# Large sums and scalings of an attention moved from GpSimd to DVE and ACT, and the emptying of two kinds of blocks put first in the plan

## The chip, the cores and the metric

One core of one Trainium2 chip. The metric is the device time of one execution in microseconds; the kernel before takes 782.17 us (median of 3 runs, 782.04 to 782.22).

## The reference

Two pre-norm residual layers on 256 positions of width 2048, then a final norm. The first layer is sliding-window attention (window 128, 32 query heads on 4 key/value heads, a learned sink per head in the softmax's denominator). The second has three attention branches on one set of queries: over 15 compressed blocks, over selected blocks (with 256 positions all blocks are selected), and over a window that covers all positions; each branch's result is weighted with a sigmoid gate per head. Both multiply the attention's output with a SiLU gate before the output projection.

```python
for i in range(DEPTH):                      # DEPTH = 2
    h = rmsnorm(x, norm_w[i])
    out = mixer_a(...) if i == 0 else mixer_b(...)
    x = x + out
return rmsnorm(x, final_norm_w)

# mixer_a, per head:  e = exp(s - m);  p = e / (sum(e) + exp(sink - m));  o = p @ v
# mixer_b, per head:  o = g0 * o_cmp + g1 * o_slc + g2 * o_win,  g = sigmoid(gates)
# both:               out = (o * silu(z)) @ w_out
```

## The kernel before

The kernel is written as two layers of code. `trunk` records every operation into a `Plan` and emits nothing. `Plan.order` then simulates the five engines with a price for each operation (`_price`) and a latency between engines, and sends each engine, whenever it is free in that simulation, the ready operation with the smallest `i - early`, where `i` is the place in the program. `early` is normally 0; `FIRST` puts an operation before all normal ones, `LAST` behind them. The order found in this way is the order of the instructions in each engine's queue, and on the chip each engine works through its queue in that order, waiting by semaphores. The prices know nothing of one engine holding up another. All recorded operations therefore have one line in the profile (L217, the call in `emit`), and they are told apart by the names of their tiles.

The projections are 234 weight blocks ("steps"), each a 128x1024 tile of weights. SP loads it (`raw`, 4 buffers), ACT rounds it to a high part (`w_hi`), DVE subtracts to get the low part (`w_lo`, 3 buffers each; both recorded as FIRST in `split`), and TensorE multiplies activations with the parts in three passes into one of three PSUM banks (`acc`; the matmuls are recorded as LAST, so that they fill what attention leaves). When a block of columns is done, a function empties its bank. For queries that is `post_q` (L636): ACT copies the bank to `q` with a scale, GpSimd rotates the first quarter of the head's width (`rope`). For gates it is `post_z` (L687): ACT copies one half of the bank to `side`, DVE adds it to the other half and writes `u`; from `u` a tanh and products make the SiLU gate. A bank is free for the next block when these have read it.

Attention runs beside the projections, one unit per head group (4) and tile of 128 positions (`t`, 2): a front part (transposing queries, scores, softmax) and a back part (transposing probabilities, products with the values), each cut into pieces. `background` runs pieces after each half step, against a credit that grows by a rate per half step; the rates stand in one list by stage (L1331). A unit has two parities of heads (`par`), each with four heads in one tile `sm` (128 x 4 x 256).

In the first layer (`a_scores`, L753), per unit and parity: scores (`s`) go through DVE (mask and maximum), ACT takes the exponential and its sum, DVE adds the sink's part (`es`) to `den` and takes the reciprocal. For `t` = 1 GpSimd then adds the two halves of `sm`, and for both `t` GpSimd multiplies by `den`. In the back part for `t` = 1 DVE multiplies the transposed probabilities with two masks (`pt<-pT,part`). In the second layer (`b_scores`, L1176) there are two such tiles per unit and parity, one per branch: after the exponentials, the reciprocal and the product with the gates (`denb`), DVE scales the first branch's tile and GpSimd the second's. The compressed branch's softmax (`cmp_softmax`, L1215) runs on DVE and ACT, with one product on GpSimd (`sc`), and gives `pc`. TensorE transposes `sm` into `pT`, and ACT or DVE copies that to `pt`.

Of the kernel before, what the change touches and what calls it, by code (L numbers as in the profile page):

```python
# [17 lines left out]
OP = mybir.AluOpType  # L18
AX = mybir.AxisListType

P = 128
# [10 lines left out]
FIRST, LAST = 1 << 20, -(1 << 20)  # L32
# [307 lines left out]
def trunk(ctx: ExitStack, tc: tile.TileContext, x, final_norm_w, a_w_in, a_w_out, b_w_in, kc_pos, kc_w1, kc_w2, vc_pos, vc_w1, vc_w2,  # L340
          b_w_out, consts, small, xT, out):
    nc = tc.nc
    plan = Plan()
    PE, ACT, DVE, POOL, SP = (Engine(plan, n, e) for n, e in (
        ("PE", nc.tensor), ("ACT", nc.scalar), ("DVE", nc.vector), ("POOL", nc.gpsimd), ("SP", nc.sync)))
# [7 lines left out]
    def s_bank(name):  # L353
        return pp.tile([P, NB], F32, tag="s", name=name, bufs=2)
# [7 lines left out]
    def copy(out, in_, scale=1.0):  # L362
        return ACT.activation(out, in_, AF.Copy, scale=scale)
# [258 lines left out]
    def rope(v, t, nh):  # L622

        tmp = sb.tile([P, 2, HPG, 16], F32, tag="rope", name="rope")
        a, b = tmp[:, 0, 0:nh, :], tmp[:, 1, 0:nh, :]

        def bc(tab, lo, n):
            return tab[:, t].rearrange("p a b -> p (a b)")[:, None, lo:lo + n].to_broadcast([P, nh, n])
        POOL.tensor_tensor(out=a, in0=v[:, :, 0:16], in1=bc(cs, 0, 16), op=OP.mult)
        POOL.tensor_tensor(out=b[:, :, 0:8], in0=v[:, :, 8:16], in1=bc(sn, 0, 8), op=OP.mult)  # L630
        POOL.tensor_tensor(out=b[:, :, 8:16], in0=v[:, :, 0:8], in1=bc(sn, 8, 8), op=OP.mult)
        POOL.tensor_tensor(out=v[:, :, 0:16], in0=a, in1=b, op=OP.add)
# [3 lines left out]
    def post_q(layer, g):  # L636
        def post(t, ps):
            q = sb.tile([P, NB], F32, tag="q", name="q", bufs=4)
            copy(q, ps, scale=rq[layer][:, t:t + 1])
            rope(q.rearrange("p (h d) -> p h d", d=HD), t, HPG)  # L640
            qs[layer, g, t] = q
            flags.add(("q", layer, g, t))
        return post
# [43 lines left out]
    def post_z(layer, g, part):  # L687
        def post(b, ps):
            if part == b == 0:
                us[layer, g] = sb.tile([P, 4, S], F32, tag="u", name="u", bufs=2)  # L690
            u = us[layer, g][:, 2 * part + b, :]
            side = sb.tile([P, S], F32, tag="q32", name="side", bufs=2)
            copy(side, ps[:, S:2 * S])
            DVE.tensor_tensor(u, ps[:, 0:S], side, op=OP.add)
            if b == 0:
                return
            u = us[layer, g][:, 2 * part:2 * part + 2, :]
            DVE.tensor_tensor(u, u, rbc[:, None, :].to_broadcast([P, 2, S]), op=OP.mult)
            th = sb.tile([P, 2, S], F32, tag="q32", name="th", bufs=2)
            ACT.activation(th, u, AF.Tanh)  # L700
            DVE.scalar_tensor_tensor(u, th, 1.0, u, op0=OP.add, op1=OP.mult)
            if part == 1:
                flags.add(("z", layer, g))
                urgent.extend(gated(layer, g, *held) for held in late.pop((layer, g), []))
        return post
# [21 lines left out]
    def gated(layer, g, t, pv, aT):  # L727
        u = us[layer, g][:, :, t * P:(t + 1) * P]
        DVE.tensor_tensor(u, u, pv, op=OP.mult)
        hi = aT[0][:, 4 * g:4 * g + 4, t * P:(t + 1) * P]  # L730
        copy(hi, u)
        DVE.tensor_sub(aT[1][:, 4 * g:4 * g + 4, t * P:(t + 1) * P], u, hi)
        flags.add(("a", layer, g, t))
        yield 0.0
# [18 lines left out]
    def a_scores(g, t, kT, qT, par, sm, nm, den):  # L753
        n = (t + 1) * P
        mk = mflat[:, 2 * P:2 * P + n]
        for i0 in (0, 2):
            ps = s_bank("s")
            for i in (i0, i0 + 1):
                o = ps[:, (i - i0) * S:(i - i0 + 1) * S]
                q = qT[:, 2 * i + par, :]  # L760
                if t == 0:

                    PE.matmul(o.rearrange("p (a b) -> p a b", a=2), q, kT[:, g, :, P:2 * P], start=True, stop=True)
                else:
                    for hl in range(2):
                        PE.matmul(o, q, kT[:, g, hl, 0:S], start=hl == 0, stop=hl == 1)
            if t == 0:
                sides = ps.rearrange("p (i a b) -> p i a b", i=2, a=2)
                low = sb.tile([P, 512], F32, tag="q32", name="low", bufs=2)[:, 0:2 * P].rearrange("p (i b) -> p i b", i=2)
                DVE.tensor_tensor(low, sides[:, :, 1, :], mk[:, None, :].to_broadcast([P, 2, P]), op=OP.add)  # L770
            for i in (i0, i0 + 1):
                h = g * HPG + 2 * i + par
                src, other = (sides[:, i - i0, 0, :], low[:, i - i0, :]) if t == 0 else (
                    ps[:, (i - i0) * S:(i - i0 + 1) * S], mk)
                DVE.tensor_tensor_reduce(out=sm[0][:, i, 0:n], in0=src, in1=other,
                                         scale=-1.0, scalar=nsink[:, h:h + 1], op0=OP.add, op1=OP.min,
                                         accum_out=nm[:, i:i + 1])
                ACT.activation(sm[0][:, i, 0:n], sm[0][:, i, 0:n], AF.Exp, scale=-1.0,
                               bias=nm[:, i:i + 1], accum_out=den[:, i:i + 1])
            yield 220.0 * (t + 1)  # L780
        es = sb.tile([P, 4], F32, tag="es", name="es", bufs=2)
        h0 = g * HPG + par
        DVE.tensor_tensor(es, nm, sinks[:, h0:h0 + 7:2], op=OP.add)
        ACT.activation(es, es, AF.Exp)
        DVE.tensor_tensor(den, den, es, op=OP.add)
        DVE.reciprocal(den, den)
        p = sm[0][:, :, 0:P]
        if t:

            POOL.tensor_tensor(out=p, in0=p, in1=sm[0][:, :, P:2 * P], op=OP.add)  # L790
        POOL.tensor_tensor(out=p, in0=p, in1=den[:, :, None].to_broadcast([P, 4, P]), op=OP.mult)
        yield 0.0

    def p_transposed(sms, br, off, k):
# [106 lines left out]
    nA = len(steps)  # L901
# [35 lines left out]
    nA_out = len(steps)  # L937
# [236 lines left out]
    nB = len(steps)  # L1174

    def b_scores(g, t, qT, par, sm, nm, den, sc):  # L1176
        kT = lay["kT"]
        for i in range(4):
            h = 2 * i + par
            if t == 0:  # L1180
                spans = [(128, 272)]
            else:
                spans = [(0, 272), (272, 256)]
            banks = []
            for off, n in spans:
                ps = s_bank("s")
                banks.append(ps)
                for hl in range(2):
                    PE.matmul(ps[:, 0:n], qT[:, h, :], kT[:, g, hl, off:off + n], start=hl == 0, stop=hl == 1)
            if t == 0:  # L1190
                parts = [(banks[0][:, 0:P], mflat[:, 0:P]), (banks[0][:, 144:272], mflat[:, 0:P])]
                pc = banks[0][:, P:P + 16]
            else:
                parts = [(banks[0][:, 0:S], mflat[:, 0:S]), (banks[1][:, 0:S], mflat[:, P:P + S])]
                pc = banks[0][:, S:S + 16]
            n = (t + 1) * P
            for br, (src, mk) in enumerate(parts):
                DVE.tensor_tensor_reduce(out=sm[br][:, i, 0:n], in0=src, in1=mk, scale=-1.0, scalar=-NEG,
                                         op0=OP.add, op1=OP.min, accum_out=nm[:, br, i:i + 1])
                if br == 0:  # L1200
                    DVE.tensor_tensor(sc[:, h, :], pc, mask_c[:, t, :], op=OP.add)
                ACT.activation(sm[br][:, i, 0:n], sm[br][:, i, 0:n], AF.Exp, scale=-1.0,
                               bias=nm[:, br, i:i + 1], accum_out=den[:, br, i:i + 1])
            yield 230.0 * len(spans)
        DVE.reciprocal(den, den)
        h0 = g * HPG + par
        DVE.tensor_tensor(den, den, lay["gate"][:, t, 1:3, h0:h0 + 7:2], op=OP.mult)
        n = (t + 1) * P
        for br in range(2):
            eng = POOL if br else DVE  # L1210
            eng.tensor_tensor(out=sm[br][:, :, 0:n], in0=sm[br][:, :, 0:n],
                              in1=den[:, br, :, None].to_broadcast([P, 4, n]), op=OP.mult)
        yield 0.0

    def cmp_softmax(g, t, sc):  # L1215
# [104 lines left out]
    n = len(steps)  # L1320
# [7 lines left out]
    hT_pair(0, hT0, 0)  # L1328
    for i in range(AHEAD):
        split(steps[i])  # L1330
    rates = [(0, 450.0), (nA, 900.0), (nA + 8, 600.0), (nA_out, 750.0), (nB, 1200.0)]  # L1331
    for i, st in enumerate(steps):
        for start, r in rates:
            if i == start:
# [77 lines left out]
```

## Time and profile before

| | us |
|---|---|
| median of 3 runs | 782.17 (782.04 to 782.22) |
| the profiled execution | 782.04 |
| its span, first to last instruction | 780.0 |
| TensorE (PE) busy | 766.9 |
| DVE busy | 569.6 |
| ACT busy | 469.9 |
| GpSimd (POOL) busy | 124.4 |

The granted clock of TensorE is 0.998 of full speed over the span. Matmuls are pipelined: a matmul's duration in the timeline includes the time in which its results drain, during which the next has begun, so that the time that a matmul really takes is the distance from its start to the next one's. An idle time in brackets is the engine's own, before the instruction, with what ended it. Repeated buffers of a tile carry one name.

### The profile page before, as it was taken

The numbers are of one execution on the slowest core, as the hardware profiler recorded it, in microseconds if no ns is written. First come the engines' busy times: TensorE is split into PE (matmuls) and PEld (weight loads), VectorE is DVE, ScalarE is ACT, GpSimd is POOL, SyncE is SP. The second block draws the span as 40 slices with busy tenths as digits, with TensorE's granted clock in tenths as the row PEclk, the third lists the DMA queues.
The fourth block names the chain that finished last, engine by engine and source line by source line (L and its number), as shares of the span: only waits on it lengthen the run. The fifth ranks groups of instructions, "written<-read, shape, count | busy, mean of one in ns | idle before, by whom it ended". The sixth has DMA issues, their size and how long they took to land.

```text
span 780.0 us, 11584 instructions
## 1 busy us (share of the span) xinstructions
PE 766.9 (98%) x3992; PEld 623.6 (80%) x3992; DVE 569.6 (73%) x1159; ACT 469.9 (60%) x950; POOL 124.4 (16%) x170
## 2 busy tenths in 40 slices
PE   8999999999999999999999999999999999999995
PEld 6888688787787788888888888878878887868884
DVE  6649959869779655565776579969969798965562
ACT  6857557457466445544666477667657866845442
POOL 1112112113023000020101021311232411111110
PEclk9999999999999999999999999999999999999999
DMA  9763563654554555676687653545445352454642
GB/s 326 242 207 117 162 187 111 171 181 133 164 163 134 181 184 182 186 200 171 182 245 238 176 163 109 163 113 159 122 122 149 107 158 102 135 190 155 195 164 108
DMA packets 86475, 129.73 MB, mean 166 GB/s; under 512 B 6323, under 2 KB 43234, under 8 KB 86289
## 3 DMA queue, kind: packets, MB, share of 16 engines
q1 hardware_dynamic: 85792, 127.42, 54.0%
q0 software_dynamic: 336, 1.29, 0.5%
q8 instruction: 31, 0.51, 0.3%
q10 hardware_dynamic: 288, 0.30, 0.1%
q14 instruction: 28, 0.22, 0.1%
HBM read 126.89 MB, written 2.10 MB: 165 GB/s over the span
## 4 chain that ended last, share of the span: by engine, by line
PE 83%; DVE 12%; issue 4%; DMA 1%; ACT 0%; ACTq 0%; POOLq 0%; POOL 0%; SPq 0%; DVEq 0%
PE acc L217 68%; PE pv L217 4%; DVE w_lo L217 3%; PE s L217 3%; PE pT L217 3%; DVE sm L217 3%; DVE den L217 2%; DVE u L217 1%; PE mlp L217 1%; DVE qT L217 1%; PE qT L217 1%; PE gates L217 1%; PE xT L217 1%; DMA raw<-in_a_w_in 1%; DVE pt L217 1%
## 5 line engine op out<-in xcount | busy, mean ns | idle before, releaser
L217 DVE TENSOR_TENSOR w_lo<-raw,w_hi 128x1024 fp32r<-128x1024 f32 (+1 forms) x231 | 297.0, 1288 | 141.0 <-ACT w_hi L217 137.9
L217 ACT ACTIVATE w_hi<-raw 128x1024 fp32r<-128x1024 f32 (+1 forms) x231 | 241.1, 1048 | 161.4 <-PE acc L217 123.6
L217 PE MATMUL acc<-w_hi,hT 128*128 128x512 f32 x768 | 244.4, 395 | 1.7 <-DVE u L217 1.0
L217 PE MATMUL acc<-hT,w_hi 128*128 128x512 f32 x512 | 185.0, 397 | 0.0
L217 PEld LDWEIGHTS acc<-w_hi,hT 128*128 128x128 f32 x768 | 142.2, 188 | 33.2 <-issue 2.4
L217 PE MATMUL acc<-w_lo,hT 128*128 128x512 f32 x384 | 150.4, 394 | 0.0
L217 PE MATMUL acc<-hT,w_lo 128*128 128x256 f32 x512 | 144.8, 285 | 0.0
L217 PEld LDWEIGHTS acc<-hT,w_hi 128*128 128x128 f32 x512 | 96.2, 188 | 18.1
L217 PEld LDWEIGHTS acc<-hT,w_lo 128*128 128x128 f32 x512 | 96.6, 189 | 0.7
L217 PE MATMUL acc<-w_hi,aT_hi 128*128 128x512 f32 x236 | 92.5, 393 | 0.3 <-DVE kTB L217 0.3
L217 PE MATMUL acc<-w_hi,aT_lo 128*128 128x512 f32 x236 | 92.6, 392 | 0.0
L217 PE MATMUL acc<-w_lo,aT_hi 128*128 128x512 f32 x236 | 92.1, 391 | 0.0
L217 PEld LDWEIGHTS acc<-w_lo,hT 128*128 128x128 f32 x384 | 72.0, 188 | 13.5
L217 ACT ACTIVATE sm<-sm,nmb 128x128 f32<-128x128 f32 (+1 forms) x128 | 56.7, 444 | 18.7 <-DVE nmb L217 15.4
L217 POOL TENSOR_TENSOR sm<-sm,denb 128x512 f32<-128x512 f32 (+1 forms) x16 | 31.5, 1966 | 142.3 <-DVE mx L217 32.8
L217 PEld LDWEIGHTS acc<-w_hi,aT_hi 128*128 128x128 f32 x236 | 44.2, 188 | 9.9 <-DVE kTB L217 0.8
L217 PEld LDWEIGHTS acc<-w_hi,aT_lo 128*128 128x128 f32 x236 | 44.3, 188 | 9.7 <-issue 0.8
L217 PEld LDWEIGHTS acc<-w_lo,aT_hi 128*128 128x128 f32 x236 | 44.3, 188 | 8.9
L217 DVE CUSTOM_DVE_ANT_0 sm<-s,mask 128x128 f32<-128x128 f32 (+1 forms) x128 | 42.7, 348 | 10.1 <-PE s L217 9.6
L217 PE MATMUL pT<-ident,sm 128*128 128x128 f32 x256 | 38.2, 274 | 0.6 <-DVE sm L217 0.6
L217 PEld LDWEIGHTS s<-kTB,qT 128*128 128x128 f32 x192 | 31.9, 188 | 8.2 <-issue 3.1
L217 PE MATMUL s<-kTB,qT 128*128 128x272 f32 x192 | 38.3, 295 | 0.0
(188 smaller groups left out, 864.5 us busy)
## 6 DMA issues: line engine op xcount, KB each, us to landing
raw<-in_b_w_in SPq DMA_DIRECT2D x88, 512.0 KB, 3.7
raw<-in_a_w_in SPq DMA_DIRECT2D x71, 512.0 KB, 3.7
raw<-in_a_w_out SPq DMA_DIRECT2D x32, 512.0 KB, 3.8
raw<-in_b_w_out SPq DMA_DIRECT2D x32, 512.0 KB, 4.5
x<-in_x SPq DMA_DIRECT2D x8, 256.0 KB, 7.1
raw<-in_b_cmp_k_w SPq DMA_DIRECT2D x4, 512.0 KB, 3.7
raw<-in_b_cmp_v_w SPq DMA_DIRECT2D x4, 512.0 KB, 4.1
out<-x SPq DMA_DIRECT2D x4, 512.0 KB, 3.1
```

Source lines behind the costliest of these rows:

```text
L217: return getattr(eng.real, method)(*[real(a) for a in args], **{k: real(a) for k, a in kw.items()})
```

## The change

Four things. (1) In the first layer's softmax the sum of the two halves (8 times) and the multiplication by `den` (16 times) are issued on DVE instead of GpSimd. (2) In the second layer the scaling of the second branch's tile, one GpSimd operation for four heads (16 times), becomes four ACT copies with a scale, one per head, in place. (3) In `post_q` and `post_z` the operations that empty the bank (ACT's copy to `q`; ACT's copy to `side` and DVE's sum to `u`) are recorded as FIRST. (4) The credit rate between the first layer's output projection and the second's is 800 instead of 750.

```diff
     def post_q(layer, g):
         def post(t, ps):
             q = sb.tile([P, NB], F32, tag="q", name="q", bufs=4)
+            plan.early = FIRST
             copy(q, ps, scale=rq[layer][:, t:t + 1])
+            plan.early = 0
             rope(q.rearrange("p (h d) -> p h d", d=HD), t, HPG)
...
             side = sb.tile([P, S], F32, tag="q32", name="side", bufs=2)
+            plan.early = FIRST
             copy(side, ps[:, S:2 * S])
             DVE.tensor_tensor(u, ps[:, 0:S], side, op=OP.add)
+            plan.early = 0
             if b == 0:
                 return
...
         p = sm[0][:, :, 0:P]
         if t:
 
-            POOL.tensor_tensor(out=p, in0=p, in1=sm[0][:, :, P:2 * P], op=OP.add)
-        POOL.tensor_tensor(out=p, in0=p, in1=den[:, :, None].to_broadcast([P, 4, P]), op=OP.mult)
+            DVE.tensor_tensor(out=p, in0=p, in1=sm[0][:, :, P:2 * P], op=OP.add)
+        DVE.tensor_tensor(out=p, in0=p, in1=den[:, :, None].to_broadcast([P, 4, P]), op=OP.mult)
         yield 0.0
...
         n = (t + 1) * P
-        for br in range(2):
-            eng = POOL if br else DVE
-            eng.tensor_tensor(out=sm[br][:, :, 0:n], in0=sm[br][:, :, 0:n],
-                              in1=den[:, br, :, None].to_broadcast([P, 4, n]), op=OP.mult)
+        DVE.tensor_tensor(out=sm[0][:, :, 0:n], in0=sm[0][:, :, 0:n],
+                          in1=den[:, 0, :, None].to_broadcast([P, 4, n]), op=OP.mult)
+        for i in range(4):
+            copy(sm[1][:, i, 0:n], sm[1][:, i, 0:n], scale=den[:, 1, i:i + 1])
         yield 0.0
...
-    rates = [(0, 450.0), (nA, 900.0), (nA + 8, 600.0), (nA_out, 750.0), (nB, 1200.0)]
+    rates = [(0, 450.0), (nA, 900.0), (nA + 8, 600.0), (nA_out, 800.0), (nB, 1200.0)]
```

## Rows read from the trace of the kernel before

**Rows 1.** The page's part 1: engine, busy us, share of the span, instructions.
```profile
PE 766.9 (98%) x3992; PEld 623.6 (80%) x3992; DVE 569.6 (73%) x1159; ACT 469.9 (60%) x950; POOL 124.4 (16%) x170
```

**Rows 2.** List of waits, TensorE alone: who waited for whom, us, times, longest.
```profile
PE acc L217 <- DVE u L217: 1.0, 3, 0.3
PE acc L217 <- ACT w_hi L217: 0.8, 1, 0.8
...
PE acc L217 <- DVE kTB L217: 0.3, 1, 0.3
PE pcT L217 <- DVE pc L217: 0.3, 1, 0.3
```

**Rows 3.** Timeline, 82.4 to 86.4 us: start, duration, engine, line, operation [idle before].
```profile
82.54 1.22 DVE L217 TENSOR_TENSOR w_lo<-raw,w_hi 128x1024 fp32r<-128x1024 f32 x1
...
82.85 2.05 POOL L217 TENSOR_TENSOR sm<-sm 128x512 f32<-128x512 f32 x1 [5.74 <-ACT sm L217]
...
83.67 1.25 DVE L217 TENSOR_TENSOR den<-den,es 128x4 f32<-128x4 f32 x1
...
84.52 0.36 ACT L217 ACTIVATE side<-acc 128x256 f32<-128x256 f32 x1
...
84.81 0.62 PE L217 MATMUL acc<-w_hi,hT 128*128 128x512 f32 x2
84.85 0.68 DVE L217 TENSOR_TENSOR pt<-pT,part 128x512 f32<-128x512 f32 x1
...
85.27 0.40 PE L217 MATMUL acc<-w_lo,hT 128*128 128x512 f32 x1
85.45 0.16 DVE L217 RECIPROCAL den<-den 128x4 f32<-128x4 f32 x1
85.54 0.39 DVE L217 TENSOR_TENSOR u<-acc,side 128x256 f32<-128x256 f32 x1
...
85.85 2.03 DVE L217 TENSOR_TENSOR w_lo<-raw,w_hi 128x1024 fp32r<-128x1024 f32 x1
...
85.98 0.73 PE L217 MATMUL acc<-w_hi,hT 128*128 128x512 f32 x2 [0.31 <-DVE u L217]
```

**Rows 4.** Timeline of DVE alone, 66 to 75 us.
```profile
68.83 1.77 DVE L217 TENSOR_TENSOR w_lo<-raw,w_hi 128x1024 fp32r<-128x1024 f32 x1
...
71.94 0.16 DVE L217 TENSOR_TENSOR den<-den,es 128x4 f32<-128x4 f32 x1
```

**Rows 5.** Timeline, 670 to 674 us and 682 to 687 us.
```profile
670.08 2.89 DVE L217 TENSOR_TENSOR w_lo<-raw,w_hi 128x1024 fp32r<-128x1024 f32 x1
...
673.59 0.40 PE L217 MATMUL acc<-w_hi,aT_hi 128*128 128x512 f32 x1
...
682.11 2.25 POOL L217 TENSOR_TENSOR sm<-sm,denb 128x1024 f32<-128x1024 f32 x1 [2.43 <-DVE mx L217]
...
682.52 2.92 DVE L217 TENSOR_TENSOR w_lo<-raw,w_hi 128x1024 fp32r<-128x1024 f32 x1
...
685.36 1.21 DVE L217 TENSOR_TENSOR sm<-sm,denb 128x1024 f32<-128x1024 f32 x1
...
685.67 0.39 PE L217 MATMUL acc<-w_hi,aT_lo 128*128 128x512 f32 x1
...
686.63 0.77 PE L217 MATMUL pT<-ident,sm 128*128 128x128 f32 x5 [0.57 <-DVE sm L217]
```

**Rows 6.** Groups of instructions by form, ACT's: xcount | busy us, mean ns | idle.
```profile
L217 ACT ACTIVATE hT<-xf,small 128x256 fp32r<-128x256 f32 x8 | 3.6, 496 | 2.0 <-DMA small<-in_small 2.0
...
L217 ACT ACTIVATE pc<-sc 128x256 fp32r<-128x256 f32 x8 | 3.3, 414 | 7.9 <-POOL sc L217 7.8
...
L217 ACT ACTIVATE sc<-sc 128x128 f32<-128x128 f32 x8 | 2.4, 298 | 0.7 <-DVE sc L217 0.7
```

**Rows 7.** Windows: stretch, us, busy of PE, PEld, DVE, ACT, POOL, clock, DMA.
```profile
60.00:92.00 32.00, 31.69 (x175) 24.55 (x173) 31.01 (x74) 21.37 (x55) 7.50 (x6) 1.00 0.45 132
...
460.00:500.00 40.00, 40.00 (x223) 32.95 (x223) 36.76 (x118) 30.47 (x86) 5.77 (x5) 1.00 0.49 140
```

## The prediction

> **What bounds the kernel now.** The first view is the page's busy times: TensorE is busy for 766.9 of 780.0 us, DVE 569.6, ACT 469.9, GpSimd 124.4 [rows 1]. So TensorE's stream sets the end, and a change on the other engines is worth only what it takes from TensorE's waits or adds to them. The second view is therefore the list of TensorE's waits [rows 2]: behind the start-up there is little. It waits for the query/gate emptying `u` (1.0 us in 3 times), for `kTB` once (0.3), for the compressed probabilities `pc` (0.3). That list counts only idle time in which no earlier matmul still drains, so I priced each wait in the timeline from start to start. At 85.27 a matmul starts, and the next at 85.98, against 0.23 us where nothing waits (two from 84.81 to 85.27): 0.71 - 0.23 = 0.48 us [rows 3]. This place comes once in each of the first layer's four head groups, the first three naming `u` and the fourth `kTB`: 4 x 0.48 = 1.9 us. At 685.67 a matmul starts and the next at 686.63, behind `sm`: 0.96 - 0.23 = 0.73 us [rows 5]. The `pc` wait and its surroundings are at most the 0.3 us of its row plus what the drain hides, as `u` shows (0.31 idle stands for 0.48), so 0.46 us. Everything of the attention that TensorE visibly loses is 1.9 + 0.73 + 0.46 = 3.1 us. That is the prize, and it is small.
>
> The third view is what made those waits late: DVE's and GpSimd's rows just before them. The same 128x4 `den<-den,es` takes 0.16 us at 71.94 and 1.25 us at 83.67, while GpSimd's 128x512 sum runs from 82.85 to 84.90 [rows 3, 4]. DVE's `w_lo` takes 2.03 us at 85.85 beside GpSimd's scaling (82.54: 1.22 us) [rows 3]. At 682.52 a `w_lo` takes 2.92 us beside the 2.25 us scaling that starts at 682.11, and only after it does DVE start the scaling that TensorE waits for [rows 5]. So a large GpSimd operation does not run beside DVE's operations with two inputs in SBUF: one stands still.
>
> **The change, part by part.** (1) First layer: 8 sums and 16 scalings of 128x512 leave GpSimd for DVE. DVE pays 0.60 us for each, start to start (84.85 to 85.45) [rows 3], so 24 x 0.60 = 14.4 us. What it gets back: in one group's stretch six DVE operations are stretched: `w_lo` at 68.83 by 0.55 (1.77 instead of 1.22), `es` at 73.34 by 0.2, `den` at 74.46 by 1.1, `u` at 76.28 by half of its 1.39, `den` at 83.67 by 1.1, `w_lo` at 85.85 by 0.8 [rows 3, 4]; together about 4.5 us a group, 18 us in four. The net is 3.6 - 4.5 = -0.9 us a group: DVE's load hardly moves, in a stretch where it is busy for 31.01 of 32 us [rows 7]. But where the time lies does move. Between 83.67 and the `u` at 85.54 DVE now spends 1.18 on the held `den`, 0.60 on `pt`, 0.09 on the reciprocal; after, 0.10 for `den`, then sum, `pt`, reciprocal and scaling, 0.10 + 3 x 0.60 + 0.09 = 1.99: no earlier by itself.
>
> (2) That is what the third part decides. Emptying gets first place in the plan: `u` needs only its `side`, which ACT ends at 84.88 [rows 3], so it can start behind whatever DVE holds then (one 0.60 us operation as a rule), at 85.0 to 85.5 instead of 85.54. TensorE wants the bank at 85.50 and `u` takes 0.39. I take the wait as gone: -4 x 0.48 = -1.9 us, with ends 0 (`u` comes no earlier) and -2.3 (0.11 us more each, since the pair behind the wait took 0.73 against 0.62 [rows 3]). What is late next are the sum and the scaling that `u` passes, by 0.33 us; their reader, the transposes, is planned with other matmuls before it, so 0. The query copy on ACT passes others in the same way; the weight splits queued behind it wait for 0.6 us, and TensorE waited for `w_hi` once in the run, at the start [rows 2]. Both put 0 to the sum. The rotation on GpSimd that follows the query copy only gains room. No DMA is moved.
>
> (3) Second layer: 16 scalings (8 of 512, 8 of 1024 elements) leave GpSimd for ACT, as 64 copies with a scale from memory, 32 of 128 and 32 of 256 elements. No such row exists. From above, 128x256 with a scale pointer is 496 ns; from below, without pointers, `sc` 128x128 is 298 and `pc` 128x256 is 414 [rows 6]; for 128x128 the upper end is then 298 + 82 = 380. So 32 x (0.298 + 0.414) = 22.8 us to 32 x (0.380 + 0.496) = 28.0. I take the lower end, as neighbours on ACT overlap a little. In the stretch where they come ACT is busy for about three quarters (30.47 of 40 us [rows 7]), so they fit on average. DVE gains between the 1.7 us twice that are shown (2.89 and 2.92 against 1.22 [rows 3, 5]) and 16 x 1.7 = 27 us. None of it is on TensorE's path except at 682: without GpSimd's scaling that `w_lo` takes 1.2 instead of 2.9 us, and the scaling behind it starts 1.7 us earlier than 685.36. That is more than the 0.73 us that TensorE waited: -0.73, with ends 0 and -0.73. For the `pc` wait, whose multiplication stays on GpSimd, I take half: -0.2 (ends 0 and -0.46).
>
> (4) The rate 800 instead of 750 between the second layer's first and last projections hands out background work 6.7% sooner. TensorE's work is the same, so 0; it leaves less attention for the last projection, which is where the 0.73 us was lost. And a new order of everything may make or lose waits; with nothing in the trace to size it I bound it by half of what there is, 1.5 us either way.
>
> The Trainium skill speaks against the direction of (1): "Perfetto Trace Analysis", Optimizing Scalar/DVE Operations, advises moving work off a saturated DVE, to Scalar or even GPSIMD, and joining operations on a saturated engine; by it a DVE at 97% should not take 14.4 us more. The same section adds that GPSIMD and DVE share a port, so that moves between them might not help. The rows here side with the second half.
>
> **The sum.** -1.9 - 0.73 - 0.2 = -2.8 us. The profiled execution is 782.04 us, 2.04 more than its span, and the median 782.17: about 779.2.
>
> **The rivals.** First, DVE stays the bound of the first layer's attention. For it: 31.01 of 32 us busy [rows 7] and a net relief of 0.9 us a group. Then `u` or a `w_lo` is late by the same 0.5 us a group, four times, and only the end's 0.73 and 0.2 are gained: 782.1 - 0.9 = 781.2. The same comes out if giving the emptying first place does nothing, as it sorts only operations that are ready at the same planned time, and `u` may be late only by what is already running. Against it: the 1.1 us hold sits just before the wait [rows 3]. The advice of the Trainium skill's "Perfetto Trace Analysis", named above, describes this case.
>
> Second, and slower: ACT's copies come as bursts ahead of the weight splits. A burst for the second token tile is 4 x 0.41 = 1.6 us in ACT's queue; if a `w_hi` is queued behind it, its `w_lo` on DVE and then TensorE are later by as much. A narrow place: `w_lo` from 670.08 ends at 672.97, and its first matmul starts at 673.59, a lead of 0.62 us [rows 5] (by counting, the 203rd of 234 weight blocks). Where the lead is below 1.6, a burst costs up to 1.0 us. Three such places, with the first layer's gain kept: 782.1 - 1.9 + 3 x 1.0 = 783.2; all 8 bursts: 788. Against it: that same lead was 1.7 us shorter through GpSimd, which is now away, and splits have first place in the plan.
>
> Third, the plan's prices now meet what happens (it never knew of the holds), and more small delays go than I count: 782.1 - 3.1 - 0.4 - 1.5 = 777.1.
>
> **How the numbers follow.** Forecast and its neighbours down to 777 have 0.63 (the third case 0.12 of it), the first rival 0.21, the second 0.16. The range reaches from 777.0 to 783.4: it takes in the first rival and the three-place form of the second. A measurement of this kernel can tell about 0.2%, 1.6 us. Faster by more than that 0.63, within it 0.21, slower 0.16.
>
> **What would show it.** Right: no wait of TensorE for `u` or `kTB` at the end of a head group; no `den<-den,es` above 0.2 us; no `w_lo` near 2.9 us in the second layer; DVE's busy time lower by some 17 us (an estimate: 3.6 in the first layer, half of 27 in the second), ACT's higher by 20 to 28. Wrong: new TensorE waits for `w_lo` or `w_hi` (second rival), `u` still named at the four places (first), or `pT` waiting for ACT's scaled `sm`, which would mean that the four copies come later than GpSimd's single pass did.

## The result, and the profile after

The changed kernel takes 775.40 us (median, 775.36 to 775.55) against 782.17: a ratio of 0.9915, 95% interval 0.9904 to 0.9925. That is faster by 6.8 us, where 2.8 were forecast, and it lies below the range (777.0 to 783.4). The profiled execution is 775.40 us, its span 773.5 against 780.0.

The page after, busy time by engine:

```profile
PE 762.5 (99%) x3992; PEld 624.2 (81%) x3992; DVE 553.5 (72%) x1183; ACT 492.9 (64%) x1014; POOL 59.2 (8%) x130
```

Against [rows 1] DVE is busy 16.1 us less (forecast: some 17; by the stretches named below it is 2.3 in the first, where 3.6 were forecast, and 13.9 in the second, where 13.5 were) and ACT 23.0 more (20 to 28), GpSimd half as long as before. TensorE's busy time falls by 4.4 us with the same 3992 matmuls. So most of the gain was not idle time to begin with, and no list of waits could show it whole.

TensorE's list of waits in after, which answers [rows 2] (who waited for whom, us, times, longest):

```profile
PE idle L217 <- DVE warm L217: 1.3, 1, 1.3
PE acc L217 <- ACT w_hi L217: 0.6, 1, 0.6
PE acc L217 <- ACT q L217: 0.2, 1, 0.2
```

The first two belong to the start-up. `u`, `kTB` and `pc` are gone, and so is the wait for `sm` of [rows 5]; one for the query copy `q` is new.

The groups of instructions by form, DVE's and ACT's (xcount | busy us, mean ns | idle before), show the holds going. First before, the rows that the tables ahead of the prediction don't have:

```profile
L217 DVE TENSOR_TENSOR w_lo<-raw,w_hi 128x1024 fp32r<-128x1024 f32 x225 | 292.6, 1302 | 139.5 <-ACT w_hi L217 136.5 <-PE kcT L217 1.4
...
L217 DVE TENSOR_TENSOR u<-u,rbc 128x512 f32<-128x512 f32 x16 | 13.8, 864 | 0.4
...
L217 DVE TENSOR_TENSOR den<-den,es 128x4 f32<-128x4 f32 x16 | 11.3, 704 | 0.7 <-ACT es L217 0.6
```

The same view of after, with the moved operations in their new place:

```profile
L217 DVE TENSOR_TENSOR w_lo<-raw,w_hi 128x1024 fp32r<-128x1024 f32 x225 | 277.6, 1236 | 139.8 <-ACT w_hi L217 136.6 <-PE kcT L217 1.4 <-PE acc L217 0.4
...
L217 ACT ACTIVATE sm<-sm,denb 128x256 f32<-128x256 f32 x32 | 13.9, 497 | 0.0
...
L217 DVE TENSOR_TENSOR u<-u,rbc 128x512 f32<-128x512 f32 x16 | 10.9, 684 | 0.1
L217 DVE TENSOR_TENSOR sm<-sm,den 128x512 f32<-128x512 f32 x16 | 10.9, 683 | 0.0
...
L217 ACT ACTIVATE sm<-sm,denb 128x128 f32<-128x128 f32 x32 | 10.1, 389 | 0.0
...
L217 DVE TENSOR_TENSOR den<-den,es 128x4 f32<-128x4 f32 x16 | 2.5, 157 | 0.7 <-ACT es L217 0.6
```

The 128x4 sum falls from 704 to 157 ns (of the two durations in [rows 3] and [rows 4] only the short one is left), and `u<-u,rbc` from 864 to 684. These two groups give back 8.8 and 2.9 of the 16.4 us that 24 operations of 0.683 cost DVE. An ACT copy takes 497 and 389 ns, near the upper ends (496 and 380, from [rows 6]). But neighbours overlap, as the prediction had assumed: 32 of 497 ns are 15.9 us, of which ACT is busy 13.9, and both forms together keep it busy for 24.0 us, near the lower end of 22.8 that was taken.

Where the 6.5 us of the span lie can be read from three start times on TensorE: the first transposes of queries in the first layer (55.99 before, 55.95 after), the second layer's first transposes of `x` (272.23, 267.76) and the last matmul (770.72, 764.25). Between the first two it is 4.43 us shorter, between the last two 2.00. These two stretches, "first" and "second", serve for every run below, always as the difference from before's 216.24 and 498.49 us in the profiled execution.

### The profile page after: what moved, and what is told of

Same layout as the page of the kernel before. It is cut to its first block, busy times and chain, and to the rows that moved or that the text cites. A ratio compares the mean times of both kernels' runs of the same rounds, so it can differ in the third digit from the quotient of the medians.

```text
span 773.5 us, 11558 instructions
## 1 busy us (share of the span) xinstructions
PE 762.5 (99%) x3992; PEld 624.2 (81%) x3992; DVE 553.5 (72%) x1183; ACT 492.9 (64%) x1014; POOL 59.2 (8%) x130
## 4 chain that ended last, share of the span: by engine, by line
PE 96%; issue 1%; DMA 1%; ACT 0%; DVE 0%; ACTq 0%; POOLq 0%; POOL 0%; SPq 0%
PE acc L217 79%; PE pv L217 5%; PE s L217 5%; PE pT L217 4%; PE mlp L217 1%; PE qT L217 1%; PE gates L217 1%; PE xT L217 1%; DMA raw<-in_a_w_in 1%; PE kT L217 0%; PE pcT L217 0%; PE kcT L217 0%; PE hid L217 0%; ACT junk L217 0%; PE cmp L217 0%
## 5 line engine op out<-in xcount | busy, mean ns | idle before, releaser
L217 DVE TENSOR_TENSOR w_lo<-raw,w_hi 128x1024 fp32r<-128x1024 f32 (+1 forms) x231 | 282.0, 1224 | 141.8 <-ACT w_hi L217 138.6
L217 PEld LDWEIGHTS acc<-w_lo,hT 128*128 128x128 f32 x384 | 72.0, 188 | 13.5
L217 PEld LDWEIGHTS pT<-ident,sm 128*128 128x128 f32 x256 | 30.8, 140 | 4.1
```

What stands on the lines that cost most here:

```text
L217: return getattr(eng.real, method)(*[real(a) for a in args], **{k: real(a) for k, a in kw.items()})
```

## The experiments

| run | what it is | median us | ratio [95%] | first | second |
|---|---|---|---|---|---|
| after | all four parts | 775.40 | 0.9915 [0.9904, 0.9925] | -4.43 | -2.00 |
| e1 | before + DVE sums and scalings (1) | 779.70 | 0.9970 [0.9959, 0.9982] | -1.40 | -0.12 |
| e2 | before + emptying first (3) | 787.95 | 1.0072 [1.0059, 1.0085] | -1.47 | +7.72 |
| e3 | before + ACT copies (2) | 781.06 | 0.9987 [0.9978, 0.9996] | -0.06 | -0.68 |
| e4 | before + rate 800 (4) | 781.67 | 0.9995 [0.9986, 1.0004] | 0 | -0.1 |
| e5 | after without (1) | 778.19 | 0.9951 [0.9938, 0.9963] | -1.49 | -2.00 |
| e6 | after without (3) | 779.82 | 0.9972 [0.9961, 0.9982] | -1.38 | -0.84 |
| e7 | after without (2) | 781.46 | 0.9993 [0.9984, 1.0002] | -4.43 | +4.64 |
| e8 | after without (4) | 778.52 | 0.9958 [0.9946, 0.9971] | -4.43 | +2.48 |
| e9 | before, one copy moved | 779.23 | 0.9963 [0.9949, 0.9977] | -2.52 | +0.04 |
| e10 | before + (1) and (3), first layer alone | 778.12 | 0.9950 [0.9937, 0.9962] | -4.43 | -0.14 |
| e11 | after at rate 850 | 775.32 | 0.9914 [0.9901, 0.9928] | -4.43 | -2.0 |
| e12 | after + unread work on GpSimd | 778.64 | 0.9955 [0.9943, 0.9968] | -1.02 | -2.0 |
| e13 | e7 at rate 900 | 784.09 | 1.0020 [1.0011, 1.0028] | -4.43 | +6.8 |
| e14 | e2 at rate 900 | 787.20 | 1.0055 [1.0041, 1.0069] | -1.47 | +7.2 |

The numbers (1) to (4) are the change's own. A kernel's profiled execution is not always at its median: that of e8 took 780.08 us, and its "second" holds 1.5 us that four of its five executions don't have (half clock; the last section), and the "second" of e2, e13 and e14 holds about as much of it. e1 gains a further 0.67 us before the first stretch, where its code is before's. In the other runs the start-up lies within 0.15 us of before's; the reason is open, and nothing is built on it.

**One part at a time.** e1:

```diff
-            POOL.tensor_tensor(out=p, in0=p, in1=sm[0][:, :, P:2 * P], op=OP.add)
-        POOL.tensor_tensor(out=p, in0=p, in1=den[:, :, None].to_broadcast([P, 4, P]), op=OP.mult)
+            DVE.tensor_tensor(out=p, in0=p, in1=sm[0][:, :, P:2 * P], op=OP.add)
+        DVE.tensor_tensor(out=p, in0=p, in1=den[:, :, None].to_broadcast([P, 4, P]), op=OP.mult)
```

> The kernel before with part (1) alone: the first layer's 8 sums and 16 scalings on DVE. Theory H (GpSimd's large operations hold DVE; the products with the values lose their pairing and u comes late because of these holds): both losses go, 4 x 0.48 for u and about 2.4 for the four pairs, so 782.1 - 4.4 = 777.7, and no `den<-den,es` above 0.2 us. Rival F (emptying first is what brings u in time): only the pairs come back, 782.1 - 2.4 = 779.7, and the four waits for u stay. Rival S (DVE is saturated, and the gain lies elsewhere): 781 to 783.

e2, in `post_q` and `post_z` alike:

```diff
+            plan.early = FIRST
             copy(q, ps, scale=rq[layer][:, t:t + 1])
+            plan.early = 0
```

> The kernel before with part (3) alone: bank emptying recorded as FIRST. H: u still stands behind the held `den` on DVE, so little comes of it, 781.5 to 782.3. F: the four waits for u go, 782.1 - 1.9 = 780.2, the unpaired products with the values stay.

e3 and e4:

```diff
-        for br in range(2):
-            eng = POOL if br else DVE
...
+        for i in range(4):
+            copy(sm[1][:, i, 0:n], sm[1][:, i, 0:n], scale=den[:, 1, i:i + 1])
```

> The kernel before with the second layer's scaling as 64 ACT copies alone. H: the 0.73 us before the last transposes goes and some more, 782.1 - 1 to - 2 = 780.1 to 781.1, DVE busy lower by about 14 us. Rival: the second layer's gain comes from the rate, and this run is within 0.4 us of before.

```diff
-    rates = [(0, 450.0), (nA, 900.0), (nA + 8, 600.0), (nA_out, 750.0), (nB, 1200.0)]
+    rates = [(0, 450.0), (nA, 900.0), (nA + 8, 600.0), (nA_out, 800.0), (nB, 1200.0)]
```

> The kernel before with the rate 800 alone. H: within 0.5 us of before, 781.6 to 782.6, as TensorE's work is the same. Rival: it takes the 0.73 us wait away and some, 780.5 to 781.4.

e3 and e4 come out as their H said. e1's 779.70 us is the number of its F, but by luck: 0.67 us of the gain are the start-up, and what F said of the waits for `u` is not what happened. e2 is over 5 us slower than either of its theories said, through the second layer (below). In the first stretch (1) alone gives 1.40 us and (3) alone 1.47, together 2.9; the whole change has 4.43 there. The parts don't add up, and the timelines say why. The timeline (start us, us, engine, operation, idle before) of e1 at the end of the first head group:

```profile
85.36 0.69 DVE L217 TENSOR_TENSOR sm<-sm 128x512 f32<-128x512 f32 x1
...
85.66 0.39 PE L217 MATMUL acc<-w_lo,hT 128*128 128x512 f32 x1
85.97 0.17 DVE L217 RECIPROCAL den<-den 128x4 f32<-128x4 f32 x1
86.05 0.39 DVE L217 TENSOR_TENSOR u<-acc,side 128x256 f32<-128x256 f32 x1
...
86.59 0.70 PE L217 MATMUL acc<-w_hi,hT 128*128 128x512 f32 x2 [0.55 <-DVE u L217]
```

The sum and the reciprocal stand ahead of `u`, and the wait grows: 86.59 - 85.66 - 0.23 = 0.70 us instead of the 0.48 of [rows 3], in four places 2.8 instead of 1.96. So the first rival is real where (1) stands alone. The timeline of e2 at the same point:

```profile
84.64 1.04 POOL L217 TENSOR_TENSOR sm<-sm,den 128x512 f32<-128x512 f32 x1 [0.87 <-DVE den L217]
84.75 0.40 PE L217 MATMUL acc<-w_lo,hT 128*128 128x512 f32 x1
...
85.74 0.66 PE L217 MATMUL pT<-ident,sm 128*128 128x128 f32 x4 [0.59 <-POOL sm L217]
```

`u` is no longer waited for (0.35 us once), but GpSimd's scaling now comes too late for the transposes: 85.74 - 84.75 - 0.23 = 0.76 us here, 2.7 in four. In the change neither happens; the timeline of after at that point:

```profile
82.17 0.47 DVE L217 CUSTOM_DVE_ANT_0 sm<-s,mask,nsink 128x256 f32<-128x256 f32 x1
...
82.20 0.39 ACT L217 ACTIVATE side<-acc 128x256 f32<-128x256 f32 x1 [0.52 <-PE acc L217]
...
82.62 0.42 DVE L217 TENSOR_TENSOR u<-acc,side 128x256 f32<-128x256 f32 x1
```

`u` starts with `side` hardly ended, behind one short operation. But waits alone leave e1 with a loss (0.9 us more), and it gained 1.4. Something that both e1 and e2 remove is in no list of waits.

**The hidden loss.** For the unit's first tile (`t` = 0) the back part multiplies both parities' probabilities with the values, four matmuls into two halves of the columns of a bank. TensorE's timeline at the first of them in the change:

```profile
78.96 1.08 PE L217 MATMUL pv<-pt,vA 128*64 128x512 f32 x4
79.97 0.39 PE L217 MATMUL acc<-hT,w_lo 128*128 128x256 f32 x1
```

and the timeline of before, with the other engines:

```profile
76.08 1.04 POOL L217 TENSOR_TENSOR sm<-sm,den 128x512 f32<-128x512 f32 x1 [0.38 <-DVE den L217]
...
76.28 1.39 DVE L217 TENSOR_TENSOR u<-u,rbc 128x512 f32<-128x512 f32 x1
...
77.38 2.01 PE L217 MATMUL pv<-pt,vA 128*64 128x512 f32 x4
77.59 0.68 DVE L217 COPY pt<-pT 128x512 f32<-128x512 f32 x1
...
78.32 0.19 PEld L217 LDWEIGHTS pv<-pt,vA 128*64 128x64 f32 x2 [0.75 <-DVE pt L217]
...
79.33 0.66 PE L217 MATMUL pT<-ident,sm 128*128 128x128 f32 x4
```

After, the four take 1.01 us from their start to the next one's; before 1.95, and in the three other groups 1.50, 1.49 and 1.51. The reason is a chain: GpSimd's scaling at 76.08 holds DVE's `u<-u,rbc` (1.39 instead of 0.68 us), behind which DVE's copy `pt` for the second parity starts only at 77.59; the weights of the second pair load at 78.32, when the first pair is nearly through. With both parities' `pt` there, the two pairs run side by side. The sum over four groups is 6.45 - 4 x 1.01 = 2.4 us, and TensorE counts as busy throughout. Together with the four waits (1.96) it is 4.36 of the 4.43 us of the first stretch. e1 then balances as -2.4 + 0.85 = -1.55 (measured -1.40), e2 as -2.4 - 1.96 + 0.35 + 2.7 = -1.3 (-1.47).

The holds and the order each have a part in the late `pt`. In before's own order, with neither this hold nor the one before it (`den<-den,es` at 74.46, 1.26 instead of 0.16 us), `pt` would start up to 1.8 us earlier, in time for the first pair at 77.38: an estimate from these rows. In e2 GpSimd keeps its operations, and DVE is still held, but the new order has `pt` ahead of the hold, as its timeline shows:

```profile
76.89 0.68 DVE L217 COPY pt<-pT 128x512 f32<-128x512 f32 x1
...
78.33 1.08 PE L217 MATMUL pv<-pt,vA 128*64 128x512 f32 x4
...
78.63 1.24 DVE L217 TENSOR_TENSOR den<-den,es 128x4 f32<-128x4 f32 x1
```

All four groups of e2 take 1.01 us. In e1 and after the order on DVE is a new one too, and no run has before's order without the holds. How much of the 2.4 us the change owes to the freed DVE and how much to the order is therefore not shown.

e9 asks for this term by itself: in before, for `t` = 0 alone, ACT copies the second parity's `pt` instead of DVE.

```diff
-            evac(par + k, pt, tb)
+            evac(0 if on_act else par + k, pt, tb)
...
-            yield from pv_blocks(sms, [(0, 0, vt[:, 0, gs])], pv, True)
+            yield from pv_blocks(sms, [(0, 0, vt[:, 0, gs])], pv, True, True)
```

> The kernel before, with one copy moved: in the first layer's first tile of positions ACT, not DVE, copies the second parity's transposed probabilities `pt`. GpSimd keeps its sums and scalings. Theory P (the matmul pairs with the values ran one after the other because DVE's `pt` was late, held behind GpSimd's scaling; TensorE's list of waits hides it under the drain): the four pairs take 1.01 instead of 1.5 to 1.94 us, 782.1 - 2.4 = 779.7, the four waits for u stay. Rival: the pairs are apart for another reason (an extra semaphore instruction of the second half), and nothing changes, 781.8 to 782.4.

The four take 1.01 us in all groups, although DVE's operations are held as before (`den` 1.26 us at 74.49, `u<-u,rbc` 1.39 at 76.31), so it is the late `pt` that keeps the pairs apart. The stretch is 2.52 shorter. The size agrees; the run is not clean, since the plan made another order, in which the four waits for `u` ended, against the expectation, and GpSimd's scaling became late for the transposes instead (`PE pT <- POOL sm`, 1.2 us in 4; start to start 1.9). -2.4 - 1.96 + 1.9 = -2.5.

**The change with a part undone.** Each is the change with the lines of one part as before.

```diff
-            DVE.tensor_tensor(out=p, in0=p, in1=sm[0][:, :, P:2 * P], op=OP.add)
+            POOL.tensor_tensor(out=p, in0=p, in1=sm[0][:, :, P:2 * P], op=OP.add)
...
```

> The changed kernel with the first layer's sums and scalings back on GpSimd. H: all of the first layer's gain is lost, 775.4 + 4.4 = 779.8, with four unpaired products and the four waits for u back. F: emptying first keeps u in time, and only the pairs are lost: 777.8.

```diff
-            plan.early = FIRST
             copy(side, ps[:, S:2 * S])
...
```

> The changed kernel without part (3). H: without the holds u is in time by itself, 775.4 to 775.9. F: the four waits for u are back, 775.4 + 1.9 = 777.3.

```diff
-        for i in range(4):
-            copy(sm[1][:, i, 0:n], sm[1][:, i, 0:n], scale=den[:, 1, i:i + 1])
+        for br in range(2):
+            eng = POOL if br else DVE
...
```

> The changed kernel with the second layer's scaling back on GpSimd. H: the second layer's gain of 2.0 us is lost wholly or mostly, 776.4 to 777.4. Rival (rate): within 0.4 us of 775.4.

```diff
-    rates = [(0, 450.0), (nA, 900.0), (nA + 8, 600.0), (nA_out, 800.0), (nB, 1200.0)]
+    rates = [(0, 450.0), (nA, 900.0), (nA + 8, 600.0), (nA_out, 750.0), (nB, 1200.0)]
```

> The changed kernel with the rate back at 750. H: within 0.5 us of 775.4. Rival (rate): 776.4 to 777.4.

Only e5's F comes near its number (777.8), and not for its reason: the pairs stay at 1.01 us, and what comes back is the transposes' wait for GpSimd's scaled `sm` (2.0 us idle in 4). e6, e7 and e8 are slower than any of their theories. e5 and e6 repeat the first stretch of e2 and e1 (-1.49, -1.38), so (1) and (3) need each other there. e7 and e8 show what the single runs could not: with emptying first, both the ACT copies and the rate carry the second layer. TensorE's waits in e7:

```profile
...
PE acc L217 <- ACT aT_hi L217: 0.9, 1, 0.9
PE pT L217 <- DVE pt L217: 0.8, 1, 0.8
PE pT L217 <- DVE sm L217: 0.7, 2, 0.6
PE s L217 <- DVE sc L217: 0.6, 1, 0.6
```

and, in its timeline, one of their causes, a scaling on DVE that takes 2.92 us beside GpSimd's, with the transposes that wait for it:

```profile
624.47 2.19 POOL L217 TENSOR_TENSOR sm<-sm,denb 128x1024 f32<-128x1024 f32 x1 [6.79 <-DVE denb L217]
...
624.82 2.92 DVE L217 TENSOR_TENSOR sm<-sm,denb 128x1024 f32<-128x1024 f32 x1
...
627.79 0.87 PE L217 MATMUL pT<-ident,sm 128*128 128x128 f32 x6 [0.57 <-DVE sm L217]
```

In after the same DVE scaling takes 1.22 us (677.46) with the ACT copies beside it. e8 loses its time at the end of the attention; its timeline there:

```profile
699.08 0.50 PE L217 MATMUL pv<-pcT,vbd 128*128 128x512 f32 x1
699.62 0.60 ACT L217 ACTIVATE o<-pv 128x512 f32<-128x512 f32 x1 [2.42 <-PE pv L217]
700.25 0.69 DVE L217 TENSOR_TENSOR u<-u,o 128x512 f32<-128x512 f32 x1 [7.39 <-ACT o L217]
700.98 0.63 ACT L217 ACTIVATE aT_hi<-u 128x512 fp32r<-128x512 f32 x1 [0.76 <-DVE u L217]
...
701.66 0.50 PE L217 MATMUL acc<-w_hi,aT_hi 128*128 128x512 f32 x1 [2.08 <-ACT aT_hi L217]
```

After the last product with the values TensorE needs the gated result of the last head group, through the three operations shown, and has nothing else to do: 96 of the last projection's weight loads lie between that projection's first matmul (667.52) and this point, and without the last group's rows no more can run (six weight blocks of 12 matmuls without the last group's share, two half blocks and one more, after which the three `w_hi` buffers are full). In after 75 lie there, TensorE still has projection to do, and no wait appears in TensorE's timeline:

```profile
694.05 0.50 PE L217 MATMUL pv<-pcT,vbd 128*128 128x512 f32 x1
694.39 0.40 PE L217 MATMUL acc<-w_hi,aT_hi 128*128 128x512 f32 x1
```

**The first layer alone, and the rate further.**

```diff
+            plan.early = 0 if layer else FIRST
             copy(q, ps, scale=rq[layer][:, t:t + 1])
+            plan.early = 0
...
+        DVE.tensor_tensor(out=p, in0=p, in1=den[:, :, None].to_broadcast([P, 4, P]), op=OP.mult)
```

> The kernel before with parts (1) and (3) in the first layer alone; the second layer as before. Theory I (the two parts need each other: sums on DVE bring the pairs back but leave u late, emptying first brings u in time but with GpSimd the transposes then wait for the scaled sm): first layer -4.4, second layer 0, so 777.7. Rival: the second layer moves with it through the order, 775 to 777 or 779 and above.

```diff
+    rates = [(0, 450.0), (nA, 900.0), (nA + 8, 600.0), (nA_out, 850.0), (nB, 1200.0)]
```

> The changed kernel with the rate 850. Theory T (a threshold: with emptying first the projections run ahead, and at 750 the last unit's attention is left without matmuls to fill; 800 is enough): 775.4 +- 0.6. Rival (a slope: every 50 is worth about 3 us): 772 to 774.

e10 has the whole first stretch (-4.43) and nothing in the second: the two layers are separate. (Its median is 0.5 us above what that gives; it spends 0.88 us more than before behind the last matmul, the reason of which is open.) e11 is no slope: 850 is no better than 800. But it tests less than it seems to: the instructions of e11 stand on every engine in the same order as those of after. So the rate no longer changes the plan from 800 to 850, and what a still earlier attention would be worth is not shown.

**GpSimd's own time, or its hold on DVE?** A scaling of 128x512 on GpSimd is both slower (1.04 us in the first layer, 1.45 to 1.55 in the second, against 0.68 on DVE) and in DVE's way. e12 keeps the changed kernel's sums and scalings on DVE and adds, at their old places, 24 GpSimd products of 128x512 from constants and `es` or `den` into a tile that nothing reads.

```diff
+            POOL.tensor_tensor(out=spare, in0=mask, in1=es[:, :, None].to_broadcast([P, 4, P]), op=OP.mult)
             DVE.tensor_tensor(out=p, in0=p, in1=sm[0][:, :, P:2 * P], op=OP.add)
+        POOL.tensor_tensor(out=spare, in0=mask, in1=den[:, :, None].to_broadcast([P, 4, P]), op=OP.mult)
         DVE.tensor_tensor(out=p, in0=p, in1=den[:, :, None].to_broadcast([P, 4, P]), op=OP.mult)
```

> The changed kernel with 24 more GpSimd operations in the first layer that nobody reads, of the size and at the places of those that were moved (mask times es or den into a spare tile). Theory H (the holds of DVE are the cost): with the moved work on DVE and the holds back, the first layer loses most of its 4.4 us or more, 778 to 781, with `den` or `w_lo` stretched again. Rival L (it was GpSimd's longer way to the data: 1.04 instead of 0.60 us and a hop between engines): 775.2 to 775.8.

The timeline of e12 near 88 us:

```profile
87.86 1.66 POOL L217 TENSOR_TENSOR spare<-mask,es 128x512 f32<-128x512 f32 x1 [4.28 <-ACT es L217]
...
88.54 1.00 DVE L217 TENSOR_TENSOR den<-den,es 128x4 f32<-128x4 f32 x1
...
90.37 1.04 POOL L217 TENSOR_TENSOR spare<-mask,den 128x512 f32<-128x512 f32 x1 [0.85 <-DVE den L217]
...
90.73 1.23 DVE L217 TENSOR_TENSOR sm<-sm,den 128x512 f32<-128x512 f32 x1
...
92.02 0.66 PE L217 MATMUL pT<-ident,sm 128*128 128x128 f32 x4 [0.28 <-DVE sm L217]
```

On TensorE, DVE and ACT the instructions of e12 stand in the very order of after, so that only the work on GpSimd differs. Work that nobody waits for costs 3.4 of the 4.43 us, nearly all of it at the transposes (`PE pT <- DVE sm`, 1.5 us idle in 5; by start times 3.3 us more than in after). A hold alone is enough to cost TensorE time. "SBUF — State Buffer", Who interferes with whom, in the Trainium skill, says that a DVE operation with two SBUF inputs contends with a GpSimd operation that reads SBUF, over ports that are an exclusive lock. The 128x4 sum at 1.00 us against 0.157 agrees, and it ends when GpSimd's operation does (89.54 and 89.52). It is not the loss of before once more: all 16 of DVE's own `sm<-sm,den` are held here (1.09 to 1.57 us against 0.68), which before doesn't have, and the pairs stay at 1.01 us. And that GpSimd's longer way costs something too is not excluded: in e2 and e5 the transposes wait for its scaling itself.

**Does a higher rate replace the ACT copies?** If a late attention were all that e2 and e7 lose, 900 should cure them.

```diff
+    rates = [(0, 450.0), (nA, 900.0), (nA + 8, 600.0), (nA_out, 900.0), (nB, 1200.0)]
```

> The kernel of the seventh run (second layer's scaling on GpSimd, all else changed; 781.5 us) with the rate 900. Theory T (emptying first lets the projections run ahead of attention, and what is then left of attention at the end has no matmuls beside it; handing it out sooner repairs that, with GpSimd too): the first layer's -4.4 and about nothing in the second, 777 to 778.5. Rival W (GpSimd's holds in the second layer cost it, whatever the rate): 780.5 to 782.

> The kernel before with emptying first and the rate 900 (emptying first alone: 788.0 us). T: the second layer's loss of 7.7 us goes, the first layer's -1.4 stays, 780 to 781.5. W: most of the loss stays, 784 to 787.

It doesn't. Both come out above the ranges of both theories (the fastest executions, 782.69 us of e13 and 785.61 of e14 at a mean granted clock of 0.997 and 0.998, lie near W's range and in it). Both keep the losses between 600 and 630 us (in e13 2.5 us in three places, start to start, as in e7) and wait 2.1 us for `aT_hi`, where e7 at 800 waits 0.9. TensorE's waits in e13:

```profile
PE acc L217 <- ACT aT_hi L217: 2.1, 1, 2.1
...
PE pT L217 <- DVE pt L217: 1.0, 2, 0.8
```

and e13 has done 96 weight loads by then, as e8. That the rate alone decides is refuted. Why the attention ends late at 900 as long as GpSimd scales is open: apart from the rate, the scaling on GpSimd is what e13 has and a kernel that doesn't lose (after, or e11) has not, but it brings the holds, a slower scaling and, through its price, another order. How much each of the three does was not parted.

## Why the prediction was wrong

**The step that failed** is "Everything of the attention that TensorE visibly loses is ... 3.1 us. That is the prize". It was built from the list of waits, priced at the listed places. The unpaired products were in none of them, as TensorE was draining one pair while the other's operand was late: 2.4 us, all gained. The prediction counted the stretched `u` at 76.28 as time lost on DVE, and did not ask which TensorE operation reads what DVE does next. The span is shorter by 3.6 us more than forecast (6.5 against 2.8): 2.4 are these pairs, 1.1 the second layer.

**The four waits for `u`** were sized rightly (1.9 forecast, 1.96 gone), but put down to emptying first by itself, and the sum and scaling that `u` passes were costed at 0. In e2 their reader waits 2.7 us; it is the move to DVE that makes the 0 true. Equally part (1) was costed at nothing, and alone worsens the wait by 0.9 us. The step held only for the two together.

**The second layer** was forecast at -0.93 and gave -2.00. Both waits went whole: 0.73 us at 685.67 and 0.46 at the `pc` place, of which 0.2 had been taken; that is -1.2. The new wait for `q` gives back 0.38 start to start. The remaining 1.2 us is spread over many places that no list of waits names (a 512-column matmul of a projection is followed by a transpose of `sm` 25 times instead of 30, and so on); this was counted and not tested, and its cause stays open.

**The rate at 0** holds for before (e4: 0.9995, interval across 1). In the changed kernel it is worth 3.1 us by medians (778.52 to 775.40), since emptying first leaves the last head group late and the rate brings it back below the 96 matmuls. The prediction's bound of 1.5 us either way for "a new order of everything" was too narrow for e2, which loses 7.7 us in the second layer, some 1.5 of them to half clock.

**The second rival** did not occur where it was put. The bursts of ACT copies held up no weight split (the only `w_hi` wait is the start-up's). e3 and e6 wait 0.7 us for the query copy `q`, but no burst stands before it: in e3 it is the copy at 612.47, behind `o` (610.99) and two exponentials, with ACT idle for 1.70 us ahead of them. Before has the same three operations there (610.34, `q` at 611.82), and TensorE does not wait. Emptying first puts `q` right behind `o` (607.14 in after) and brings the wait to 0.2. So beside (2), (3) is worth 1.2 us in the second layer (e6's -0.84 against -2.00), a term that the prediction had at 0. **The first rival** occurs in e1 and not in the change. **The third** had the right direction, but its 1.9 us of small delays was a guess; the largest was one loss, the late `pt`. The mechanism itself, GpSimd holding DVE, was right: `den` at 157 ns, no `w_lo` near 2.9 us in the attention, and e12. The Trainium skill's "Perfetto Trace Analysis", Optimizing Scalar/DVE Operations, says that a saturated DVE may hand work on, even to GPSIMD. That did not decide here: DVE took 24 operations of 683 ns more, where it had been busy for 31.01 of 32 us [rows 7], and its busy time in the first stretch fell from 174.97 to 172.65 us.

## What to carry to other kernels

A list of TensorE's waits misses matmuls that could have run side by side: compare the start-to-start time of each repeated group of matmuls with its best instance, and the excess over that is part of the prize. A part whose worth hangs on another must be priced with it, by asking of each operation that is passed who reads it next. And before taking GpSimd operations as free because GpSimd is idle, look for DVE operations of the same form at two durations.

## What the runs showed of the hardware that was not expected

Two pairs of 128x64 matmuls on different halves of the columns take 1.01 us together when both operands are ready, and 1.49 to 1.95 when the second comes late; the cost is counted as busy.

A single wait of 2.1 us was followed by half clock in the profiled executions of e2, e8, e13 and e14. In e8, after the wait that ends at 701.66 (windows: us, busy of PE, PEld, DVE, ACT, POOL, clock, DMA):

```profile
699.40:701.60 2.20, 0.18 (x1) 0.00 (x0) 0.69 (x1) 1.22 (x3) 0.00 (x0) 1.00 0.00 0
...
702.40:705.50 3.10, 3.10 (x7) 2.47 (x8) 1.23 (x1) 1.16 (x2) 0.00 (x0) 0.50 0.17 42
```

From 702.40 to 705.50 the granted clock is 0.50, so 1.2 of 2.4 GHz, and matmuls follow each other at 0.43 us instead of 0.23. It does not come every time. Of e13's executions five took 782.69 to 782.90 us at a mean granted clock of 0.997 or 0.998, six 784.09 to 784.51 at 0.994 or 0.995; of e8's four 778.28 to 778.62, and the profiled one 780.08 at 0.995. So it costs some 1.5 us where it comes. That the wait brings it on is not shown: the order of events suggests it.
